# Turning queries, keys, exponentials, gates and outputs on VectorE and the DMA queue instead of TensorE, in a two-layer hybrid decoder

## The chip, the core and the metric

One core of one Trainium2 chip. The metric is the time of one execution on the device, in microseconds. The engines are named as the profile names them: PE (TensorE, matmuls and transposes by matmul), PEld (PE's weight loads), DVE (VectorE), ACT (ScalarE), POOL (GpSimd) and SP (SyncE, which here issues nearly all DMAs, in order, on one queue). Each engine runs its own instructions in one fixed order and waits on semaphores for those of the others.

## The reference

Two decoder layers over 256 positions of width 2048, all in float32. Each layer has a mixer with two kinds of heads that share one input and one output projection, then a SwiGLU feed-forward part (FFN), then a gated embedding per layer (PLE):

```
h = rms_norm(x, pre_mix_gain)
q, k, v, hq, hf, hi, hg = split(h @ w_in)          # 1024, 256, 256, 4 x 1024
attn = rms_norm(window_attention(rope(q), rope(k), v, sinks), attn_gain)
f = lb + (1 - lb) * sigmoid(hf);   k_in = (1 - lb) * sigmoid(-hf)
o = rms_norm(recurrence(silu(hq), k_in, hi, log(f)))  # 8 heads, 128 x 128 states
x += rms_norm(concat(attn, o * silu(hg)) @ w_out, post_mix_gain)
h = rms_norm(x, pre_ffn_gain)
x += rms_norm((silu(h @ w_gate) * (h @ w_up)) @ w_down, post_ffn_gain)
x += (p @ w_ple_proj) * sigmoid(rms_norm(x, ple_gain) @ w_ple_gate)
```

Attention has 16 query heads of 64 on 4 key heads, a window of 128 positions and one sink per head.

## The kernel before

**Strips.** All weights are streamed from DRAM. The unit is a *strip*: 512 columns of a weight matrix for all 256 positions, as two row tiles t = 0, 1 of 128 positions, each with an accumulator in PSUM (`acc0`, `acc1`; four buffers, so two strips). A strip of 2048 inputs comes in 8 chunks of 512 KB: `load_w` (L232) brings a chunk into `wr` (4 buffers), ACT casts it to a high part `wh` (L174), DVE makes the low part `wl` by subtraction (L175; 8 buffers of each, so one strip), and PE does 12 matmuls of 128x512 with it, 6 for each row tile: high times high (L251), low input times high (L252), high input times low (L254). So a strip is 96 matmuls. In the text below, "matmul 480" counts these weight matmuls from the start of a layer; the first layer's mixer has its strips at 0 (keys and values), 96 and 192 (queries q0, q1), then twice f, q_rec, i, g (the recurrence's two groups of heads): 288, 384, 480, 576 and 672, 768, 864, 960; from 1056 come the output projection (`w_out`), FFN and PLE. The second layer begins at 5040.

**What a strip leaves.** When a row tile is complete, `done(t, ps)` reads it from PSUM: for queries DVE multiplies it by sines and cosines (L472) and POOL adds (L479); for f, ACT writes z (L616); for q_rec ACT writes a sigmoid (L635) and DVE the product (L636), both into a `nat` buffer; g likewise (L801 to L804). The `acc` buffer of a strip is written again by the strip two places later, whose first matmul waits for these reads.

**Turning.** The next step mostly needs the data turned (positions along the free axis). Before, PE does that: four transposes by matmul with `ident` into a PSUM bank `ms` (L491 keys, L511 queries, L571 exponentials, L621 z, L644 q_rec, L189 in `split_T` for attention output, recurrence output and new x), and ACT or DVE reads the bank. In the FFN only, `shuffled` (L204) turns the hidden tile by DVE and DMAs: one DVE transpose of 32x32 blocks (L208), one DMA of 256 KB to a DRAM buffer `turn` (L211), and four DMAs of 64 KB that read the blocks back in their places (L214); `split_shuffled` then splits the result into its high and low part.

**What sets the order.** The program is written as strips in a row. `tick()` runs once a chunk; it advances the generators (attention, the recurrence's levels) by one `yield` and runs what `later(n, f)` left for n ticks hence. So the number of `yield`s and the n of `later` set after which chunk a step is issued; the tile framework's scheduler then orders each engine's instructions by priority and by when buffers and inputs come free, and puts the waits in. Engines do not reorder. SP carries the weight loads, and the turns between them.

**Attention** (`attend`, `head_pair`): per half and row tile the rotated queries are turned, scores computed (L535), then per group of four heads copied (L546) and masked (L547), reduced to the maximum (L550, L551), exponentiated by ACT four times (L554) and once for the sink (L558); the exponentials are turned and multiplied with the values (L586), the result scaled (L589).

Of the kernel before, what the change touches and what calls it, by code (L numbers as in the profile page):

```python
# [15 lines left out]
P = 128  # L16
# [30 lines left out]
def decoder(ctx: ExitStack, tc: tile.TileContext, x, p, positions, w_in, attn_sinks,  # L47
# [10 lines left out]
    np_ = ctx.enter_context(tc.tile_pool(name="np", bufs=6))  # L58
# [145 lines left out]
    def shuffled(src):  # L204


        b = nat()
        V.transpose(b.rearrange("p (q k j) -> p k q j", q=4, k=4),  # L208
                    src.rearrange("p (k q j) -> p k q j", k=4, q=4))
        m = dp.tile([4, 32, 4, P], F32, tag="turn", name="turn")  # L210
        nc.sync.dma_start(m.rearrange("a i q f -> (a i) (q f)"), b)  # L211
        d = nat()
        for q in range(4):
            nc.sync.dma_start(d[q * 32:(q + 1) * 32].rearrange("i (a f) -> i a f", a=4),  # L214
                              m[:, :, q].rearrange("a i f -> i a f"))
        return d

    def split_shuffled(d, hl, t):
        cols = slice(t * P, (t + 1) * P)
        split(d.rearrange("p (a k j) -> p k a j", a=4, k=4),  # L220
              *(a[:, :, cols].rearrange("p k (a j) -> p k a j", a=4) for a in hl))
# [223 lines left out]
    for l in range(DEPTH):  # L445
# [35 lines left out]
        def done_kv(t, ps):  # L481
# [6 lines left out]
            def turn():  # L488
                pt = bank((P, 2, P))
                for b in range(2):  # L490
                    T.transpose(pt[:, b], o[:, b * P:(b + 1) * P], ident)  # L491
                S.copy(kT[:, :, t * P:(t + 1) * P], pt)
            later(8 - t, turn)
# [12 lines left out]
        def attend(half, t, o):  # L506
            for _ in range(3):
                yield
            pt = bank((P, 4, P))
            for b in range(4):  # L510
                T.transpose(pt[:, b], o[:, b * P:(b + 1) * P], ident)  # L511
            S.copy(qT[half][:, :, t * P:(t + 1) * P], pt)
            yield
            yield from head_pair(half, t)
            if half == 1:
# [4 lines left out]
                yield  # L520
                for h in range(2):
                    split_T(blocks4(ao[t][:, h]), gain_cols(96, l, 8)[:, 4 * h:4 * h + 4], attn[h], t)

        def head_pair(half, t):
# [13 lines left out]
            for g in range(2):  # L538
# [22 lines left out]
                ex.append(s_)  # L561
# [6 lines left out]
            def turned(g):  # L568
                pt = bank((P, 4, P))
                for j in range(4):  # L570
                    T.transpose(pt[:, j], ex[g][:, j], ident)  # L571
                ec = nat((P, 4, P))
                if t == 0:
                    S.copy(ec, pt)
                    return [(t, ec)]
                ep = nat((P, 4, P))
                V.tensor_tensor(ec, pt, m_low.unsqueeze(1).to_broadcast([P, 4, P]), op=ALU.mult)
                V.tensor_tensor(ep, pt, m_up.unsqueeze(1).to_broadcast([P, 4, P]), op=ALU.mult)
# [23 lines left out]
        class Rec:  # L602
# [11 lines left out]
            def done_f(s, t, ps):  # L614
                z = nat()
                S.activation(z, ps, AF.Copy, scale=rx(t)[:, 0:1])  # L616

                def turn():
                    pt = bank((P, 4, P))
# [11 lines left out]
                later(2, turn)  # L631

            def done_q(s, t, ps):
# [6 lines left out]

                def turn():
                    pt = bank((P, 4, P))
                    for b in range(4):
                        T.transpose(pt[:, b], sg[:, b * P:(b + 1) * P], ident)  # L644
                    raw = s.qd[:, :, t, 0:P]
                    cols = slice(t * P, (t + 1) * P)
                    S.copy(raw, pt)
# [8 lines left out]
                later(3 - t, turn)  # L656
# [142 lines left out]
            def done_g(s, t, ps):  # L799
# [163 lines left out]
```

## Time and profile before

| | |
|---|---|
| median of 3 runs | 2468.09 us (2467.95 to 2470.01) |
| profiled execution | 2468.36 us |
| its span, first to last instruction | 2466.6 us, at a mean granted clock of 0.999 |
| moved by DMA | 472.40 MB, mean 192 GB/s, the queues' share 63.1% |
| weight chunks | 840 (176 for w_in, 64 w_out, 3 x 176 FFN, 64 PLE gate, 8 PLE projection), 3.8 to 4.5 us from issue to landing |
| turns (FFN only) | 40: out 256 KB, 2.7 us to landing; back 4 x 64 KB, 3.3 us |
| PSUM banks | 4 `acc`, 4 `ms` |

How to read the rows quoted below. A row of the timeline has the start and the duration in us, the engine, the line, the operation, output and inputs, the shape, and a count where equal rows were joined; in brackets the idle time before it and what ended it. A row of groups has line, engine, operation, tiles and shapes with a count, then busy us and mean ns of one, then the idle time of the engine just before them and its releaser. Matmuls are pipelined: their durations overlap, so the pace is read from their starts. A row of waits has the engine and line, what it waited for, then us in total, times, and the longest. A row of windows has for each engine the busy time and (instructions), then the granted clock of PE as a share of full speed, the DMA share and GB/s.

### The profile page before, as it was taken

What the parts mean: (1) busy time and instruction counts of PE and PEld (TensorE: products, weight loads), DVE (VectorE), ACT (ScalarE), POOL (GpSimd) and SP (SyncE); (2) the same over time, 40 slices, a digit from 0 to 9 for tenths busy, and PEclk for the clock granted to TensorE, in tenths of its full rate; (3) what the DMA queues carried; (4) which work ended last, traced back from release to release, by engine and by line L of the source; (5) the groups of instructions that cost most, each with busy time, mean ns of one, the idle gap of its engine ahead of it and who ended that gap; (6) DMA issues with size and microseconds to landing.
All of it is one profiled execution on the core that took longest, in us unless ns stands there. A gap on an engine that the chain in (4) does not pass through costs nothing.

```text
span 2466.6 us, 30888 instructions
## 1 busy us (share of the span) xinstructions
PE 2447.2 (99%) x11437; PEld 2023.1 (82%) x11437; DVE 1465.8 (59%) x1941; ACT 1186.8 (48%) x1684; POOL 101.2 (4%) x213
## 2 busy tenths in 40 slices
PE   8999999999999999999999999999999999999999
PEld 6888887888888888887888888878888888888877
DVE  7786756545555555557566867565455555555674
ACT  6655446444434444446556444464444444444463
POOL 3100001000000000001010000010000000000010
PEclk9999999999999999999999999999999999999999
DMA  8445565767667766765564454657677676677753
GB/s 258 141 142 161 153 189 162 233 192 207 215 206 209 213 209 197 225 221 158 185 202 141 139 169 144 200 173 220 189 212 222 197 212 210 209 211 211 222 173 126
DMA packets 263062, 472.40 MB, mean 192 GB/s; under 512 B 17376, under 2 KB 38784, under 8 KB 262912
## 3 DMA queue, kind: packets, MB, share of 16 engines
q1 hardware_dynamic: 262608, 470.36, 63.1%
q8 instruction: 89, 1.46, 0.2%
q14 instruction: 61, 0.50, 0.1%
q10 hardware_dynamic: 240, 0.07, 0.0%
q0 software_dynamic: 64, 0.02, 0.0%
HBM read 457.79 MB, written 12.58 MB: 191 GB/s over the span
## 4 chain that ended last, share of the span: by engine, by line
PE 95%; DMA 2%; DVE 1%; ACT 1%; issue 0%; POOL 0%; SPq 0%; ACTq 0%; DVEq 0%; POOLq 0%
PE acc L251 30%; PE acc L252 30%; PE acc L254 29%; DMA wr<-in_w_in_dram 1%; PE ms L696 1%; PE ms L586 1%; PE ms L189 1%; DVE wl L175 1%; PE ms L535 0%; ACT wh L174 0%; PE ms L733 0%; ACT junk L170 0%; PE ms L761 0%; PE ms L254 0%; PE ms L251 0%
## 5 line engine op out<-in xcount | busy, mean ns | idle before, releaser
L175 DVE TENSOR_TENSOR wl<-wr,wh 128x1024 fp32r<-128x1024 f32 x840 | 1026.8, 1224 | 897.1 <-ACT wh L174 884.1
L174 ACT CAST wh<-wr 128x1024 fp32r<-128x1024 f32 x840 | 883.9, 1054 | 1096.0 <-PE acc L252 1004.8
L251 PE MATMUL acc<-wh,ck 128*128 128x512 f32 x3328 | 1305.9, 393 | 9.2 <-ACT ck L200 5.8
L252 PE MATMUL acc<-wh,ck 128*128 128x512 f32 x3328 | 1299.1, 391 | 1.0 <-DVE ck L201 1.0
L254 PE MATMUL acc<-wl,ck 128*128 128x512 f32 x3328 | 1296.3, 390 | 0.0
L251 PEld LDWEIGHTS acc<-wh,ck 128*128 128x128 f32 x3328 | 625.1, 188 | 143.2 <-ACT ck L200 11.4
L252 PEld LDWEIGHTS acc<-wh,ck 128*128 128x128 f32 x3328 | 625.7, 188 | 133.5 <-DVE ck L201 4.9
L254 PEld LDWEIGHTS acc<-wl,ck 128*128 128x128 f32 x3328 | 624.8, 188 | 129.5
L200 ACT ACTIVATE ck<-ms,gT 128x128 fp32r<-128x128 f32 x248 | 78.9, 368 | 36.3 <-DVE ck L201 28.4
L201 DVE SCALAR_TENSOR_TENSOR ck<-ms,gT,ck 128x128 fp32r<-128x128 f32 x248 | 75.9, 346 | 20.5 <-ACT ck L200 19.9
L160 POOL TENSOR_TENSOR tiny<-ssf 128x1 f32<-128x1 f32 x4 | 2.1, 535 | 1361.2 <-ACT junk L170 1360.9
L887 DVE TENSOR_TENSOR macc<-acc,macc 128x512 f32<-128x512 f32 x48 | 33.0, 687 | 5.1 <-PE acc L254 4.5
L857 ACT ACTIVATE nat<-acc,ry 128x512 f32<-128x512 f32 x44 | 30.2, 686 | 10.7 <-PE acc L254 10.7
L170 ACT ACTIVATE junk<-x 128x512 f32<-128x512 f32 x48 | 30.3, 631 | 6.4 <-DVE x L286 4.1
L863 DVE SCALAR_TENSOR_TENSOR nat<-acc,ry,nat 128x512 f32<-128x512 f32 x44 | 32.4, 748 | 0.1
L189 PE MATMUL ms<-ident,x 128*128 128x128 f32 x192 | 27.8, 280 | 1.7 <-DVE x L920 1.3
L189 PEld LDWEIGHTS ms<-ident,x 128*128 128x128 f32 x192 | 22.6, 143 | 8.1 <-DVE x L920 2.4
L175 DVE TENSOR_TENSOR ck<-nat,ck 128x512 fp32r<-128x512 f32 x42 | 28.8, 686 | 0.0
L208 DVE STREAM_TRANSPOSE nat<-nat 128x512 f32<-128x512 f32 x40 | 28.1, 703 | 0.0
L174 ACT CAST ck<-nat 128x512 fp32r<-128x512 f32 x42 | 26.0, 619 | 4.0 <-DVE nat L181 3.6
L479 POOL TENSOR_TENSOR nat<-nat 128x256 f32<-128x256 f32 (+1 forms) x24 | 22.8, 973 | 106.6 <-DVE nat L472 50.2
L554 ACT ACTIVATE nat<-nat,tiny 128x128 f32<-128x128 f32 x64 | 24.8, 389 | 3.9 <-DVE tiny L551 3.6
(199 smaller groups left out, 871.0 us busy)
## 6 DMA issues: line engine op xcount, KB each, us to landing
wr<-in_w_in_dram SPq DMA_DIRECT2D x176, 512.0 KB, 3.8
wr<-in_w_ffn_gate_dram SPq DMA_DIRECT2D x176, 512.0 KB, 4.4
wr<-in_w_ffn_up_dram SPq DMA_DIRECT2D x176, 512.0 KB, 4.5
wr<-in_w_ffn_down_dram SPq DMA_DIRECT2D x176, 512.0 KB, 4.3
wr<-in_w_out_dram SPq DMA_DIRECT2D x64, 512.0 KB, 3.9
wr<-in_w_ple_gate_dram SPq DMA_DIRECT2D x64, 512.0 KB, 4.3
turn<-nat SPq DMA_DIRECT2D x40, 256.0 KB, 2.7
nat<-turn SPq DMA_DIRECT2D x160, 64.0 KB, 3.3
```

The costliest lines, as they stand in the source:

```text
L170: S.activation(j[:, 0:shape[1]], src, AF.Square, accum_out=acc)
L174: a = S.copy(hi, src)
L175: v = V.tensor_tensor(lo, src, hi.bitcast(F32), op=ALU.subtract)
L189: T.transpose(ps[:, b], blk, ident)
L200: marks["x"] = S.activation(h[:, b], ps[:, b], AF.Copy, scale=g)
L201: V.scalar_tensor_tensor(lo[:, b], ps[:, b], g, h[:, b].bitcast(F32), op0=ALU.mult, op1=ALU.subtract)
L251: T.matmul(ps[t], xh, hi[:, k], start=first, stop=False)
L252: T.matmul(ps[t], xl, hi[:, k], start=False, stop=False)
L254: marks[t, c] = T.matmul(ps[t], xh, lo[:, k], start=False, stop=last)
L857: S.activation(gate[t], ps, AF.Silu, scale=rx2(t)[:, 0:1])
L863: V.scalar_tensor_tensor(gate[t], ps, rx2(t)[:, 0:1], gate[t], op0=ALU.mult, op1=ALU.mult)
L887: V.tensor_tensor(m, ps, m, op=ALU.add)
```

## The change

`shuffled` takes a width of n blocks and returns the turned tile as a view of blocks, and 66 more tiles go through it instead of PE: the keys (4, n = 2), the rotated queries (8), the exponentials (16), z of f (8), the gate and query product of q_rec (8), the attention output (8), the recurrence's output (8), and in the first layer three of the four column blocks of the new x (6). The turns rise from 40 to 106, and 256 PE transposes go (10984 PE matmuls before, 10728 after). The readers of the turned tiles (copies, masks, sigmoids, splits with gain) now read `nat` buffers in SBUF instead of PSUM. Steps are issued some ticks later: queries 5 ticks after the rotation instead of 3, z 4 instead of 2, q_rec 5 - t instead of 3 - t, attention output 5 instead of 1, recurrence output 4 instead of 2, the new x 5 - t instead of 2 - t; in `head_pair` a `yield` moves ahead of the masking. `nat` has 9 buffers instead of 6. The lines of the changed file are 2 to 11 higher than those before in the parts quoted (L251, L252, L254 become L261, L262, L264).

```diff
-    np_ = ctx.enter_context(tc.tile_pool(name="np", bufs=6))
+    np_ = ctx.enter_context(tc.tile_pool(name="np", bufs=9))
...
-    def shuffled(src):
+    def shuffled(src, n=4):
-        b = nat()
-        V.transpose(b.rearrange("p (q k j) -> p k q j", q=4, k=4),
-                    src.rearrange("p (k q j) -> p k q j", k=4, q=4))
-        m = dp.tile([4, 32, 4, P], F32, tag="turn", name="turn")
+        b = nat((P, n * P))
+        V.transpose(b.rearrange("p (q k j) -> p k q j", q=4, k=n),
+                    src.rearrange("p (k q j) -> p k q j", k=n, q=4))
+        m = dp.tile([4, 32, 4, n * 32], F32, tag="turn", name="turn")
         nc.sync.dma_start(m.rearrange("a i q f -> (a i) (q f)"), b)
-        d = nat()
+        d = nat((P, n * P))
         for q in range(4):
             nc.sync.dma_start(d[q * 32:(q + 1) * 32].rearrange("i (a f) -> i a f", a=4),
                               m[:, :, q].rearrange("a i f -> i a f"))
-        return d
+        return d.rearrange("p (a k j) -> p k a j", a=4, k=n)
...
+    def split_shuffled(d, gcols, hl, t):
+        h, lo = (quarters(a[:, :, t * P:(t + 1) * P]) for a in hl)
+        if gcols is None:
+            split(d, h, lo)
+            return
+        for b in range(4):
+            g = gcols[:, b:b + 1]
+            marks["x"] = S.activation(h[:, b], d[:, b], AF.Copy, scale=g)
+            V.scalar_tensor_tensor(lo[:, b], d[:, b], g, h[:, b].bitcast(F32),
+                                   op0=ALU.mult, op1=ALU.subtract)
...
         def attend(half, t, o):
-            for _ in range(3):
+            d = shuffled(o)
+            for _ in range(5):
                 yield
-            pt = bank((P, 4, P))
-            for b in range(4):
-                T.transpose(pt[:, b], o[:, b * P:(b + 1) * P], ident)
-            S.copy(qT[half][:, :, t * P:(t + 1) * P], pt)
+            S.copy(quarters(qT[half][:, :, t * P:(t + 1) * P]), d)
             yield
             yield from head_pair(half, t)
...
-                yield
+                d = [shuffled(ao[t][:, h]) for h in range(2)]
+                for _ in range(5):
+                    yield
                 for h in range(2):
-                    split_T(blocks4(ao[t][:, h]), gain_cols(96, l, 8)[:, 4 * h:4 * h + 4], attn[h], t)
+                    split_shuffled(d[h], gain_cols(96, l, 8)[:, 4 * h:4 * h + 4], attn[h], t)
...
-                ex.append(s_)
+                ex.append(shuffled(s_.rearrange("p j k -> p (j k)")))
...
-            p0 = turned(0)
             yield
+            p0 = masked(0)
             yield
             values(0, p0)
-            p1 = turned(1)
-            yield
+            p1 = masked(1)
             yield
             values(1, p1)
...
                 z = nat()
                 S.activation(z, ps, AF.Copy, scale=rx(t)[:, 0:1])
+                d = shuffled(z)
                 def turn():
-                    pt = bank((P, 4, P))
-                    for b in range(4):
-                        T.transpose(pt[:, b], z[:, b * P:(b + 1) * P], ident)
                     cols = slice(t * P, (t + 1) * P)
-                    S.activation(s.f[:, :, cols], pt, AF.Sigmoid)
-                    S.activation(s.k[:, :, cols], pt, AF.Sigmoid, scale=-1.0)
+                    S.activation(quarters(s.f[:, :, cols]), d, AF.Sigmoid)
+                    S.activation(quarters(s.k[:, :, cols]), d, AF.Sigmoid, scale=-1.0)
...
-                later(2, turn)
+                later(4, turn)
...
-                later(3 - t, turn)
+                later(5 - t, turn)
...
-                later(2, lambda: split_T(blocks4(o), gain_cols(112, l, 8)[:, 4 * s.grp:4 * s.grp + 4],
-                                         mix[c], t))
+                d = shuffled(o)
+                later(4, lambda: split_shuffled(d, gain_cols(112, l, 8)[:, 4 * s.grp:4 * s.grp + 4],
+                                                mix[c], t))
...
+                    d = shuffled(xr[t][s]) if s < 3 else None
                     def turn(xT=nxT, ss=nss, g=gain_cols(0, l + 1, 16)):
-                        next_in(t, s, xT, g)
+                        if s < 3:
+                            split_shuffled(d, g[:, 4 * s:4 * s + 4], xT[s], t)
+                        else:
+                            next_in(t, s, xT, g)
                         square_sum(xr[t][s], ss[t][:, s:s + 1])
-                    later(3 if s == 3 else 2 - t, turn)
+                    later(3 if s == 3 else 5 - t, turn)
```

**Where instructions move, first place.** ACT's order in the first layer around the reading of z (`nat_1344`, `nat_1367` before; `nat_1408`, `nat_1425` in the changed kernel) from the accumulators of the f strip. Before:

```order
L554 ACTIVATE nat_1264,tiny_1270<-nat_1264,tiny_1267 128x128 x4
L558 ACTIVATE tiny_1275<-tiny_1275 128x4
L574 COPY nat_1303<-ms_1298 128x512
L174 CAST wh_1622<-wr_1620 128x1024
L616 ACTIVATE nat_1344<-acc0_1043,rx0_531 128x512
L174 CAST wh_1640<-wr_1638 128x1024
L574 COPY nat_1365<-ms_1360 128x512
L170 ACTIVATE junk_1358,ssa0_152<-ao0_150 128x256
L616 ACTIVATE nat_1367<-acc1_1044,rx1_557 128x512
```

In the changed kernel, where `wh_1961` is the eighth chunk of the i strip (480 to 576):

```order
L174 CAST wh_1961<-wr_1959 128x1024
L552 COPY nat_1328<-ms_1308 128x512
L560 ACTIVATE nat_1328,tiny_1334<-nat_1328,tiny_1331 128x128 x4
L564 ACTIVATE tiny_1339<-tiny_1339 128x4
L552 COPY nat_1371<-ms_1309 128x512
L560 ACTIVATE nat_1371,tiny_1377<-nat_1371,tiny_1374 128x128 x4
L564 ACTIVATE tiny_1382<-tiny_1382 128x4
L619 ACTIVATE nat_1408<-acc0_1086,rx0_531 128x512
L619 ACTIVATE nat_1425<-acc1_1087,rx1_566 128x512
```

Before, the cast next to z (`wh_1622`, the seventh chunk of the strip after f) takes a buffer that the f strip itself frees. Now the exponentials of q1's second row tile and the cast of `wh_1961` come first, and that cast takes the buffer of the eighth chunk of the q_rec strip, last read by matmul 478.

**Second place.** ACT's order around the sigmoid of q_rec (L635 before, L637 now), first layer. Before:

```order
L200 ACTIVATE ck_144<-ms_1576,gT_101 128x128
L200 ACTIVATE ck_146<-ms_1589,gT_101 128x128
L635 ACTIVATE nat_1650<-acc0_1369,rx0_531 128x512
L174 CAST wh_1899<-wr_1897 128x1024
L635 ACTIVATE nat_1660<-acc1_1370,rx1_557 128x512
```

In the changed kernel (`nat_1573`, `nat_1582`, `nat_1640` and `nat_1649` are the four turned tiles of the attention output; `wh_2213` takes the buffer that matmul 574 frees):

```order
L174 CAST wh_2195<-wr_2193 128x1024
L229 ACTIVATE ck_144<-nat_1573,gT_101 128x128 x4
L174 CAST wh_2213<-wr_2211 128x1024
L229 ACTIVATE ck_146<-nat_1582,gT_101 128x128 x4
L229 ACTIVATE ck_144<-nat_1640,gT_101 128x128 x3
L637 ACTIVATE nat_1702<-acc0_1436,rx0_531 128x512
L229 ACTIVATE ck_144<-nat_1640,gT_101 128x128
L229 ACTIVATE ck_146<-nat_1649,gT_101 128x128 x3
L637 ACTIVATE nat_1721<-acc1_1437,rx1_566 128x512
```

L635 stood behind splits that read PSUM banks; L637 stands behind splits that read tiles brought by DMA, and behind a later cast.

**Third place.** SP's order in the changed kernel between z and the attention output (`turn_1412` and `turn_1429` are z's, `turn_1571` and `turn_1580` the attention output's first two); before, this stretch of SP's order holds weight loads (L232) alone:

```order
L211 DMA turn_1389<-nat_1387 128x512
L214 DMA nat_1391<-turn_1389 32x4x128 x4
L211 DMA turn_1412<-nat_1410 128x512
L214 DMA nat_1414<-turn_1412 32x4x128 x4
L211 DMA turn_1429<-nat_1427 128x512
L242 DMA wr_2124<-in_w_in_dram 128x2x512
L214 DMA nat_1431<-turn_1429 32x4x128 x4
L242 DMA wr_2175<-in_w_in_dram 128x2x512
L242 DMA wr_2193<-in_w_in_dram 128x2x512
L211 DMA turn_1571<-nat_1569 128x512
L214 DMA nat_1573<-turn_1571 32x4x128 x4
L211 DMA turn_1580<-nat_1578 128x512
```

A read (L214) waits for its own turn's L211 to land, and all that is behind it in the queue waits with it.

More of the change, by code (lines that the diff above doesn't have):

```diff
@@ L486, in done_kv @@
             S.activation(vv[:, t], ps[:, 256:512], AF.Copy, scale=rx(t)[:, 0:1])
[L488 to L493, printed above, removed]
+            d = shuffled(o[:, 0:256], 2)
+            later(8 - t, lambda: S.copy(quarters(kT[:, :, t * P:(t + 1) * P]), d))
         def done_q(half):
@@ L639, in done_q @@
                     s.qd = sp.tile([P, 4, NT, P + 64], F32, tag="D", name="qd")
+                d = shuffled(sg)
                 def turn():
-                    pt = bank((P, 4, P))
-                    for b in range(4):
-                        T.transpose(pt[:, b], sg[:, b * P:(b + 1) * P], ident)
                     raw = s.qd[:, :, t, 0:P]
                     cols = slice(t * P, (t + 1) * P)
-                    S.copy(raw, pt)
+                    S.copy(quarters(raw), d)
                     def odd(a):
@@ L868, in done_up @@
                     d = shuffled(gate[t])
-                    later(3, lambda: split_shuffled(d, hl, t))
+                    later(3, lambda: split_shuffled(d, None, hl, t))
                 strip(xT, w_ffn_gate[l], col, done_gate, skew=SKEW if ff0 + j == 0 else 0)
```

19 lines of the change are left out of this document (7 added, 12 removed).

## The prediction

> **What bounds the kernel now.** I read the page first: the busy shares, the granted clock and the chain that ended last, then PE's own waits.
>
> ```profile
> PE 2447.2 (99%) x11437; PEld 2023.1 (82%) x11437; DVE 1465.8 (59%) x1941; ACT 1186.8 (48%) x1684; POOL 101.2 (4%) x213
> ...
> PEclk9999999999999999999999999999999999999999
> ...
> PE 95%; DMA 2%; DVE 1%; ACT 1%; issue 0%; POOL 0%; SPq 0%; ACTq 0%; DVEq 0%; POOLq 0%
> ...
> PE acc L251 <- ACT ck L200: 5.8, 9, 1.3
> PE acc L251 <- ACT wh L174: 3.3, 1, 3.3
> ```
>
> The reader is to see that PE hardly ever waits: 2447.2 of 2466.6 us busy, 95% of the chain, and the two largest of its waits are 5.8 and 3.3 us in all. So whatever leaves PE is a gain in full, and whatever makes PE wait is a loss in full; there is no slack on PE that could hide either. DVE (59%) and ACT (48%) have room in sum. What matters is where, in their fixed order, they stand when PE asks for something.
>
> **What leaves PE.** The order of the changed kernel has 256 PE matmuls fewer, all of them transposes: 62 groups of four and 4 groups of two (the keys). Their price is read from the starts of the neighbours.
>
> ```profile
> 84.17 0.39 PE L251 MATMUL acc<-wh,ck 128*128 128x512 f32 x1
> 84.40 0.39 PE L252 MATMUL acc<-wh,ck 128*128 128x512 f32 x1
> 84.63 0.40 PE L254 MATMUL acc<-wl,ck 128*128 128x512 f32 x1
> 84.86 0.60 PE L571 MATMUL ms<-ident,nat 128*128 128x128 f32 x4
> 85.22 0.48 PE L251 MATMUL acc<-wh,ck 128*128 128x512 f32 x1
> 85.54 0.39 PE L252 MATMUL acc<-wh,ck 128*128 128x512 f32 x1
> ...
> 62.49 0.40 PE L251 MATMUL acc<-wh,ck 128*128 128x512 f32 x1
> 62.72 0.41 PE L491 MATMUL ms<-ident,nat 128*128 128x128 f32 x2
> 62.88 0.48 PE L252 MATMUL acc<-wh,ck 128*128 128x512 f32 x1
> 63.20 0.39 PE L254 MATMUL acc<-wl,ck 128*128 128x512 f32 x1
> ```
>
> Weight matmuls follow each other every 0.228 us (84.17, 84.40, 84.63). With four transposes between, the second matmul after them starts at 85.54; without them it would be 84.63 + 2 x 0.228 = 85.09, so a group of four costs 0.45 us. A group of two costs 63.20 - (62.49 + 2 x 0.228) = 0.25 us. Gain: 62 x 0.45 + 4 x 0.25 = **28.9 us**.
>
> [...]
>
> **What is added, and lies beside PE.** 66 turns: each is one DVE transpose, one DMA out and four DMAs back.
>
> ```profile
> L208 DVE STREAM_TRANSPOSE nat<-nat 128x512 f32<-128x512 f32 x40 | 28.1, 703 | 0.0
> 457.99 0.34 SPq L211 DMA_DIRECT2D turn<-nat  x1
> 459.09 0.37 SPq L232 DMA_DIRECT2D wr<-in_w_ffn_up_dram  x1
> 461.17 1.76 SPq L214 DMA_DIRECT2D nat<-turn  x4
> DMA to landing us min/median/max: 1.8/3.3/6.2
> ```
>
> DVE: 62 x 0.703 + 4 x about 0.36 = 45 us, which takes it from 59% to 61%. SP: a turn is issued at 457.99, its last read at 461.17 + 1.76 = 462.9, so a turn holds the queue some 4.9 us (with one weight load in between; I take 4.6 without it), and its data are there about 2 us after that. This lies beside PE wherever nobody asks for it sooner. I cost the keys, both outputs of the recurrence, the new x and the second recurrence group at nothing: the matmuls until their reader hide them (the last turned output, `mix[3]`, is read 1128 + 13 matmuls into a layer, 85 matmuls or 19 us behind its strip, against 17 for reading that strip, two turns in series (9.2), their landing and the splits). Were this cover 5 us short, each layer would lose 5 us more. The weight loads between the turns keep their lead: 20 turns of one attention stage are 92 us of SP, and PE takes 87 us for its 384 matmuls before any stall.
>
> **What PE will wait for.** Each `acc` pair is used again two strips later, so a strip of PE cannot start before ACT or DVE has read the strip two before it. In the orders above these reads have moved behind work that itself waits for PE. The durations:
>
> ```profile
> L175 DVE TENSOR_TENSOR wl<-wr,wh 128x1024 fp32r<-128x1024 f32 x840 | 1026.8, 1224 | 897.1 <-ACT wh L174 884.1
> L174 ACT CAST wh<-wr 128x1024 fp32r<-128x1024 f32 x840 | 883.9, 1054 | 1096.0 <-PE acc L252 1004.8
> ...
> L554 ACT ACTIVATE nat<-nat,tiny 128x128 f32<-128x128 f32 x64 | 24.8, 389 | 3.9 <-DVE tiny L551 3.6
> ...
> L546 ACT COPY nat<-ms 128x512 f32<-128x512 f32 x8 | 4.2, 570 | 0.0
> L547 DVE COPY_PREDICATED nat<-m_prev,ms 128x512 f32<-128x512 int32 x8 | 5.5, 736 | 0.4
> L550 DVE TENSOR_REDUCE tiny<-nat 128x4 f32<-128x512 f32 x16 | 10.8, 677 | 0.0
> L616 ACT ACTIVATE nat<-acc,rx 128x512 f32<-128x512 f32 x8 | 5.5, 684 | 3.1 <-PE acc L254 3.1
> L472 DVE TENSOR_TENSOR nat<-acc,rot 128x512 f32<-128x512 f32 x16 | 10.4, 685 | 2.7 <-POOL nat L479 1.9 <-PE acc L254 0.4 <-issue 0.3
> L635 ACT ACTIVATE nat<-acc,rx 128x512 f32<-128x512 f32 x8 | 5.5, 686 | 1.1 <-PE acc L254 1.1
> L636 DVE SCALAR_TENSOR_TENSOR nat<-acc,rx,nat 128x512 f32<-128x512 f32 x8 | 6.0, 745 | 0.0
> L200 ACT ACTIVATE ck<-ms,gT 128x128 fp32r<-128x128 f32 x248 | 78.9, 368 | 36.3 <-DVE ck L201 28.4
> ```
>
> The L174 row says what ACT is doing: 1004.8 us of its idle time end with a matmul, because a cast needs the buffer of eight chunks earlier, one strip. So ACT is never ahead of PE by more than that, and everything behind a cast in its order waits with it. Positions below count a layer's weight matmuls.
>
> *The i strip (480) waits for z.* In the order, `L619` stands behind the cast of `wh_1961`, whose buffer matmul 478 frees. From there: cast 1.05, then on DVE wl 1.22, predicated copy 0.74, reduction 0.68 and a small minimum 0.16, four exponentials 1.55 (they overlap a little), in sum 5.4; then on DVE their transpose 0.70, two small ones 0.34 and again predicated copy, reduction and minimum, 1.58; then four exponentials 1.55, the small one behind them 0.19 and z itself 0.68: 10.4 us, less the two matmuls that PE still has: **10 us**, in either layer. Before, z was read as soon as it was there:
>
> ```profile
> 123.33 0.69 ACT L616 ACTIVATE nat<-acc,rx 128x512 f32<-128x512 f32 x1 [1.07 <-PE acc L254]
> 156.10 0.68 ACT L635 ACTIVATE nat<-acc,rx 128x512 f32<-128x512 f32 x1
> ```
>
> 33 us before PE came to the i strip (which follows the row at 156.10). That slack is what is gone; no transfer is part of this chain, so no DMA speed can mend it.
>
> *The q_rec strip (384) waits for the rotation of q1.* Its two reads (L472, in the changed file L482) stand in DVE's order behind the wl split that matmul 383 releases. In the second layer that is 1.22 + 2 x 0.685 = **2.6 us**; in the first the predicated copy, reduction, exponentials and transpose stand between as well, + 0.74 + 0.68 + 0.16 + 1.55 + 0.19 + 0.70 + 0.34 = 4.4: **7.0 us**.
>
> *The g strip (576) waits for the gate of q_rec.* `L637` stands in ACT's order behind the splits (L229) of the turned attention output. Floor, if every turn has landed: the cast that matmul 574 releases 1.05, seven splits 2.6, L637 0.69, L638 0.75, less 0.46 = 4.6 us. Other end: when the i strip starts, SP has six turns to do, on the last of which L637 waits, in series 6 x 4.6 = 27.6 us, and by the order there are about 9 us of gaps between them, since the attention output can only be scaled and transposed after the values, the sigmoids of f and k and four wl splits on DVE. With the landing (1.8) and the rest (2.5) that is 41 us after the start of the i strip; PE is there after 96 x 0.228 + four groups of values (3.4) + small waits, 27 to 28 us. So 4.6 to 13 us; I take **12**, near the walk's end, as the gaps are instructions with known durations.
>
> *Smaller ones:* values and scores of q1 wait for the turned q1 and exponentials (427 to 436) 3.5 and 2.0 us, the values at 523 to 532 1 us, the rest to 636 1 us per layer; between nothing and twice that.
>
> Per layer: 7.0 + 3.5 + 10 + 1 + 12 + 1 = 34.5 in the first, 2.6 + 2.0 + 10 + 1 + 12 + 1 = 28.6 in the second, **63.1 us**.
>
> **The clock after a stall.** The start of this trace has one long wait:
>
> ```profile
> 9.35 0.80 PE L251 MATMUL acc<-wh,ck 128*128 128x512 f32 x1 [3.31 <-ACT wh L174]
> 9.94 0.63 PE L252 MATMUL acc<-wh,ck 128*128 128x512 f32 x1
> 10.37 0.63 PE L251 MATMUL acc<-wh,ck 128*128 128x512 f32 x1
> ...
> 9.00:12.00 3.00, 2.65 (x6) 2.16 (x7) 2.45 (x2) 1.97 (x4) 2.03 (x35) 0.52 1.04 382
> 12.00:15.00 3.00, 3.00 (x17) 2.51 (x16) 1.36 (x2) 2.78 (x6) 0.00 (x0) 0.91 1.08 346
> ```
>
> After 3.31 us of idling the granted clock is 0.52 and matmuls start every 0.43 us, until 12.5: about eight of them at 0.2 us extra, 1.6 us. What is lost after the stall at 480 only shortens the one at 576, so I count it once per layer: **3.2 us**. [...]
>
> **Sum.** Against the profiled execution, 2468.36 us (span 2466.6 and 1.8 around it): - 28.9 + 63.1 + 3.2 = + 37.4, so 2505.8; the median of the runs is 0.3 lower: **2505.5 us**.
>
> **Rivals.** *Floor only:* turns land in time, 576 costs 4.6 and the small waits vanish: 7.0 + 2.6 + 20 + 9.2 + 3.2 - 28.9 = + 13, 2481 us. The FFN's 40 turns speak for it, on which no row of PE's waits hangs; the six turns in a row speak against it. *Faster:* the casts do not hold ACT and DVE at 383, 478 and 574, because they have run further ahead of PE than one strip when they come to these places; then only transfers are waited for, 4.6 at 576 and about 5 at 427 to 436 and around per layer: 19 - 28.9 = - 10, 2458 us. It decides at the cast before z: is it done before matmul 478 ends? The 1004.8 us above speak against it. *All of the gain*, no new wait: 2439 us; it needs every read of `acc` to be early, which the order contradicts. *Weights starve:* with 6 us per turn (the longest landing was 6.2) 20 turns are 120 us of SP against the stage's 115 (87 and its stalls), and loads behind them come late by some 10 us a layer: 2525 us. That the change doesn't do what it says: the order has no transposes left at these lines.
>
> **Chances.** Forecast 0.52, floor 0.20, faster 0.12, all of the gain 0.05, starving 0.11. The range leaves out the whole gain and the outer part of the last: 2460 to 2526 us. 0.2% (5 us) is about what measurement can tell from no change here: faster 0.15, same 0.05, slower 0.80.
>
> **What would show it.** PE's waits, now 14 us, list `acc` waiting for L619 (about 20 us in two long waits of 10) and for L638 (two of 9 to 13), and L482 in the first layer near 7; the granted clock dips behind each. PE busy falls by about 29. If L619 is not among the waits, the reading of the order is wrong, and the time is below 2470; if PE waits for wh or wl by tens of microseconds, the weights starve.

## The result, and the profile after

| | before | after |
|---|---|---|
| median, each of 4 runs on one chip | 2468.02 us (2467.07 to 2470.01) | 2520.97 us (2518.12 to 2526.50) |
| ratio after to before | | 1.0216, interval 1.0204 to 1.0228 |
| profiled execution, its span | 2468.36, 2466.6 us | 2519.89, 2518.2 us |
| mean granted clock | 0.999 | 0.987 |

So the change makes the kernel 2.2% slower; the forecast was 2505.5 with slower as the likeliest side. Of the page of the changed kernel, first the busy times, then the granted clock in 40 slices:

```profile
PE 2439.8 (97%) x11181; PEld 2008.5 (80%) x11181; DVE 1507.0 (60%) x2007; ACT 1189.0 (47%) x1684; POOL 95.9 (4%) x213
...
PEclk9998999999999999999999899999999999999999
```

PE has 256 matmuls fewer and yet only 7.4 us less of busy time (2447.2 before). It idles 2518.2 - 2439.8 = 78 us where it idled 19. Two slices, one in each layer's mixer, have a lower clock. Next PE's waits in the changed kernel (what waits, for what; us in total, times, longest):

```profile
PE acc L261 <- DVE nat L638: 23.3, 2, 11.7
PE acc L261 <- ACT nat L619: 20.6, 2, 10.3
PE acc L261 <- DVE nat L482: 11.2, 2, 7.7
PE acc L261 <- ACT ck L200: 6.1, 9, 1.3
PE acc L261 <- ACT wh L174: 3.1, 1, 3.1
PE ms L541 <- ACT qT L516: 2.2, 2, 1.8
PE acc L261 <- ACT ck L229: 2.2, 2, 1.9
```

The first three rows are new, each with one wait in each layer: 55.1 us together. All waits of this view add up to 73 us, against 14 before: + 59. With PE's - 7.4 that is the whole difference of the spans, + 51.6. No row speaks of late weights (`wh` stands there with its one wait at the start, 3.1 us), so the queue's extra turns did not starve the stream. On the timeline of the changed kernel the waits stand at the first matmuls of the strips at 384, 480 and 576, in the first layer and in the second:

```profile
120.69 0.77 PE L261 MATMUL acc<-wh,ck 128*128 128x512 f32 x1 [7.71 <-DVE nat L482]
...
125.65 0.39 PE L261 MATMUL acc<-wh,ck 128*128 128x512 f32 x1
...
165.25 0.80 PE L261 MATMUL acc<-wh,ck 128*128 128x512 f32 x1 [10.28 <-ACT nat L619]
...
206.53 0.80 PE L261 MATMUL acc<-wh,ck 128*128 128x512 f32 x1 [11.59 <-DVE nat L638]
...
1364.69 0.76 PE L261 MATMUL acc<-wh,ck 128*128 128x512 f32 x1 [3.50 <-DVE nat L482]
...
1409.06 0.79 PE L261 MATMUL acc<-wh,ck 128*128 128x512 f32 x1 [10.28 <-ACT nat L619]
...
1449.84 0.79 PE L261 MATMUL acc<-wh,ck 128*128 128x512 f32 x1 [11.73 <-DVE nat L638]
```

Behind the first of them PE needs 125.65 - 120.69 = 4.96 us for 12 matmuls that take 12 x 0.228 = 2.74 at full pace: 2.2 us more are lost after the wait has ended. Why z (L619) is late can be read from ACT's own timeline, ahead of the wait that ends at 165.25:

```profile
154.78 1.04 ACT L174 CAST wh<-wr 128x1024 fp32r<-128x1024 f32 x1 [1.67 <-PE acc L262]
155.73 0.58 ACT L552 COPY nat<-ms 128x512 f32<-128x512 f32 x1
158.67 0.40 ACT L560 ACTIVATE nat<-nat,tiny 128x128 f32<-128x128 f32 x1 [2.36 <-DVE tiny L557]
...
160.32 0.56 ACT L552 COPY nat<-ms 128x512 f32<-128x512 f32 x1
162.88 0.40 ACT L560 ACTIVATE nat<-nat,tiny 128x128 f32<-128x128 f32 x1 [2.00 <-DVE tiny L557]
...
164.53 1.47 ACT L619 ACTIVATE nat<-acc,rx 128x512 f32<-128x512 f32 x2
```

This is the chain of the prediction: a cast that waited for PE's own matmul, then two head groups' maxima and exponentials, each of which waits for DVE, and only then the two reads of z, for which PE stands still. The strip whose sums they are had ended at about 113, where PE's wait of 7.71 us begins, 51.5 us earlier; before the change the strip ended at 124.6 and ACT read its first tile at 123.3, as soon as that was complete.

In the FFN, which has the same 40 turns in both kernels, nothing is gained or lost: matmul 1440 of the program starts 28.9 us later than before, and so does matmul 4320. Behind the first layer's PLE, where the new x is turned, it is 26.0 (matmul 5040); the second layer's mixer adds the rest (51.5 at 6240, 51.6 at the last).

### The profile page after: what moved, and what is told of

It is laid out like the page before. It is cut to its first block, busy times and chain, and to the rows that moved or that the text cites. A ratio compares the mean times of both kernels' runs of the same rounds, so it can differ in the third digit from the quotient of the medians.

```text
span 2518.2 us, 30982 instructions
## 1 busy us (share of the span) xinstructions
PE 2439.8 (97%) x11181; PEld 2008.5 (80%) x11181; DVE 1507.0 (60%) x2007; ACT 1189.0 (47%) x1684; POOL 95.9 (4%) x213
## 4 chain that ended last, share of the span: by engine, by line
PE 91%; DMA 3%; ACT 2%; DVE 2%; issue 1%; SPq 0%; POOL 0%; ACTq 0%; DVEq 0%; POOLq 0%
PE acc L261 29%; PE acc L262 29%; PE acc L264 28%; DMA wr<-in_w_in_dram 1%; DMA turn<-nat 1%; PE ms L697 1%; PE ms L590 1%; DMA nat<-turn 1%; DVE wl L175 1%; ACT wh L174 1%; PE ms L541 1%; ACT nat L560 0%; PE ms L734 0%; PE ms L189 0%; ACT junk L170 0%
## 5 line engine op out<-in xcount | busy, mean ns | idle before, releaser
L175 DVE TENSOR_TENSOR wl<-wr,wh 128x1024 fp32r<-128x1024 f32 x840 | 1025.1, 1224 | 853.5 <-ACT wh L174 850.4
L261 PE MATMUL acc<-wh,ck 128*128 128x512 f32 x3328 | 1307.6, 394 | 67.0 <-DVE nat L638 23.3
L262 PE MATMUL acc<-wh,ck 128*128 128x512 f32 x3328 | 1304.6, 392 | 0.9 <-DVE ck L201 0.8
L264 PE MATMUL acc<-wl,ck 128*128 128x512 f32 x3328 | 1299.7, 391 | 0.0
L261 PEld LDWEIGHTS acc<-wh,ck 128*128 128x128 f32 x3328 | 628.1, 189 | 209.1 <-DVE nat L638 24.2
L262 PEld LDWEIGHTS acc<-wh,ck 128*128 128x128 f32 x3328 | 628.7, 189 | 135.8 <-DVE ck L201 5.0
L264 PEld LDWEIGHTS acc<-wl,ck 128*128 128x128 f32 x3328 | 627.4, 189 | 129.5
L208 DVE STREAM_TRANSPOSE nat<-nat 128x512 f32<-128x512 f32 (+1 forms) x84 | 58.2, 693 | 38.3 <-ACT nat L560 22.6
L200 ACT ACTIVATE ck<-ms,gT 128x128 fp32r<-128x128 f32 x160 | 50.2, 370 | 14.8 <-DVE ck L201 7.0
L201 DVE SCALAR_TENSOR_TENSOR ck<-ms,gT,ck 128x128 fp32r<-128x128 f32 x160 | 48.4, 346 | 14.0 <-ACT ck L200 13.6
L229 ACT ACTIVATE ck<-nat,gT 128x128 fp32r<-128x128 f32 x88 | 28.5, 390 | 32.3 <-DMA nat<-turn 32.3
L230 DVE SCALAR_TENSOR_TENSOR ck<-nat,gT,ck 128x128 fp32r<-128x128 f32 x88 | 26.3, 349 | 20.3 <-ACT ck L229 20.3
L859 ACT ACTIVATE nat<-acc,ry 128x512 f32<-128x512 f32 x44 | 30.2, 687 | 10.7 <-PE acc L264 10.7
L175 DVE TENSOR_TENSOR ck<-nat,ck 128x512 fp32r<-128x512 f32 x42 | 28.9, 687 | 0.1
```

Of the source, the lines that this page charges most:

```text
L175: v = V.tensor_tensor(lo, src, hi.bitcast(F32), op=ALU.subtract)
L200: marks["x"] = S.activation(h[:, b], ps[:, b], AF.Copy, scale=g)
L201: V.scalar_tensor_tensor(lo[:, b], ps[:, b], g, h[:, b].bitcast(F32), op0=ALU.mult, op1=ALU.subtract)
L208: V.transpose(b.rearrange("p (q k j) -> p k q j", q=4, k=n), src.rearrange("p (k q j) -> p k q j", k=n, q=4))
L261: T.matmul(ps[t], xh, hi[:, k], start=first, stop=False)
L262: T.matmul(ps[t], xl, hi[:, k], start=False, stop=False)
```

## The experiments

In these kernels a string chooses which of the added turns are made: K keys, Q queries, E exponentials, Z z, S gate and query product, A attention output, H recurrence output, X new x. A tile whose letter is missing is turned by PE, with the ticks of the kernel before; with no string shown, all are turned. All compute the whole reference. Intervals are of the ratio to the kernel before, whose median was 2468.6 us on each of the three chips used.

**The exponentials back on PE.** If the length of the chain ahead of z is the cause, taking the turn (and its two buffers) out of that chain must bring z forward.

```diff
+TURN = "KQZSAHX"
...
-                ex.append(shuffled(s_.rearrange("p j k -> p (j k)")))
+                ex.append(shuffled(s_.rearrange("p j k -> p (j k)")) if "E" in TURN else s_)
```

> Exponentials back on PE (16 turns fewer), all else as changed. By its order z now stands behind the cast that matmul 394 releases, no longer 478. Theory (PE waits at strip starts for reads that stand late in ACT's and DVE's order, and each wait costs a clock restart): the two waits of 10.3 us for z go, the rotation's 7.7 goes to about nothing, the two for q_rec's gate of 11.7 fall to 2 to 5, six clock restarts of 1.5 to 2.2 mostly go, 16 groups of 0.45 come back: about 2465 us (2458 to 2476). Rival 1 (the turns in series on SP's queue are the cause): z's chain has no transfer, so its 20.6 stay: about 2495. Rival 2 (more DVE work and DMA traffic slow everything, in proportion to the turns): 16 of 66 turns of the 82 us that the gain of 29 hides, less the gain given back: about 2508.

Measured 2464.85 us (2461.84 to 2467.51), 0.9984 [0.9974, 0.9993]: 56 us less than the changed kernel, with 16 of the 66 turns gone. Of its waits of PE:

```profile
PE acc L262 <- DVE nat L862: 4.1, 2, 2.5
...
PE acc L262 <- DVE nat L691: 1.2, 1, 1.2
```

The waits for z (now L665) and for the rotation are gone, the one for the gate (L691) is 1.2 us, and the longest new one is 2.5 us, for the recurrence's output gate (L862). So without the exponentials' turns there is no loss; the other 50 turns keep 3.8 us of the 21.7 that 46 groups of four and 4 of two are worth at the predicted prices.

**Is it the turn, or its buffers?** A turn takes two `nat` buffers beside its source: `b`, which DVE writes and the DMA reads, and `d`, into which the data come back. They can be one, since the DMAs back wait for the DMA out in any case:

```diff
-        d = nat((P, n * P))
+        d = b
```

The second kernel has this too, and splits the nine buffers: seven `nat`, and two of a tag of their own for the reads of `acc` (z, and the gate's product of q_rec).

```diff
-    np_ = ctx.enter_context(tc.tile_pool(name="np", bufs=9))
+    np_ = ctx.enter_context(tc.tile_pool(name="np", bufs=7))
...
-                z = nat()
+                z = np_.tile([P, W], F32, tag="zq", name="zq", bufs=2)
...
-                sg = nat()
+                sg = np_.tile([P, W], F32, tag="zq", name="zq", bufs=2)
```

> All turns as changed, but the data read back land in the buffer that was written out (d is b), so a turn holds one nat buffer less; still nine shared ones. By its order z stands behind the cast that matmul 442 releases. Theory: z's wait falls from 10.3 to 0 to 4, the gate's to about 6, some new waits for values: about 2488 us (2478 to 2500). Rivals 1 and 2: the same turns on the same queue, same work and traffic: 2520 us, as the changed kernel.

> As the one before (d is b), with the same nine buffers split: seven shared, two for z and q_rec's product alone. By its order z stands behind the cast that matmul 346 releases. Theory: no wait for z and none for the gate over 2 us; values and the g strip's end wait 3 to 4: about 2480 us (2470 to 2488), some 8 us under the shared nine. Rivals 1 and 2: 2520 us, no difference to the shared nine.

Measured 2489.48 us, 1.0081 [1.0066, 1.0096], with nine shared buffers, and 2458.87 us, 0.996 [0.9946, 0.9974], with seven and two: the second expectation missed, by 11 us below its lower end. Both have all 66 turns, on the same queue, and the same memory.

The first one met its time, but only in part as expected. z is waited for once (2.9), and the gate not at all, where about 6 were expected. In place of that PE waits for values (L613) and, longest, for casts of weights:

```profile
PE acc L262 <- ACT wh L175: 15.3, 3, 6.8
PE ms L626 <- ACT nat L613: 7.4, 3, 3.2
```

One of those three is the wait at the start; the others are 6.8 and 5.6 us, one in each layer. PE, ACT and the SP queue at the first of them:

```profile
186.97 0.79 PE L262 MATMUL acc<-wh,ck 128*128 128x512 f32 x1 [6.80 <-ACT wh L175]
...
185.88 1.04 ACT L175 CAST wh<-wr 128x1024 fp32r<-128x1024 f32 x1 [2.99 <-DMA wr<-in_w_in_dram]
...
172.10 7.73 SPq L215 DMA_DIRECT2D nat<-turn  x16
```

The cast waits for its weights. SP issued no weight load from 156.7 to 180.8, while six turns stood in its order, the sixteen reads of four of them in a row (in the second layer none from 1387.3 to 1409.5). That is the "weights starve" of the prediction: absent from the changed kernel, present in this one.

The split kernel's first read of z, on ACT's timeline:

```profile
108.46 0.68 ACT L665 ACTIVATE zq<-acc,rx 128x512 f32<-128x512 f32 x1
```

And of its waits of PE:

```profile
PE acc L265 <- DVE wl L176: 4.7, 2, 2.4
PE acc L262 <- DVE nat L862: 3.7, 2, 1.9
```

z is read at 108.46 where the changed kernel read it at 164.53, and neither z nor the gate of q_rec is waited for; no wait but the one at the start is above 2.5 us. The 62 us between the split and the changed kernel (31.5 for one buffer less in each turn, 30.6 for the split) are therefore not the price of transposing on DVE, nor of 66 turns on the queue as such: the buffers decide where the reads of `acc` stand, and when the turns come. The queue is not free even so. ACT's casts wait for chunks of `w_in` 7.4 us in the kernel before, 28.0 in the changed one, 61.6 with one buffer a turn and 83.3 in the split kernel, where no wait of PE for `wh` is left but the one at the start. What the orders and the profiles of six kernels say together, for the first layer (the row of the exponentials alone is an experiment further down):

| kernel | `nat` buffers, new ones per turn | turns added | z stands in ACT's order behind the cast released by matmul | f's strip ends at, us | first z read at, us | longest wait for z, us |
|---|---|---|---|---|---|---|
| before | 6, none in the mixer | 0 | 370 | 124.6 | 123.3 | none |
| changed | 9, two | 66 | 478 | 113.0 | 164.5 | 10.28 |
| exponentials on PE | 9, two | 50 | 394 | 116.2 | 132.4 | none |
| exponentials alone | 9, two | 16 | 478 | 114.5 | 152.9 | none |
| one buffer a turn | 9, one | 66 | 442 | 120.9 | 150.3 | 2.9 |
| one a turn, z apart | 7 and 2, one | 66 | 346 | 109.5 | 108.5 | none |

(A first tile is complete a little before its strip ends.) With shared buffers, z stands the later in the order, the more buffers the exponentials' turns ahead of it take: behind 478 with two each, behind 442 with one, behind 394 with none, read 51.5, 29.4 and 16.2 us after its strip's end. The number of turns does not decide: 16 turns of exponentials alone put z as far back as all 66 do. Where z has buffers of its own it is read at once. More `nat` buffers than nine were not tried.

**Only z, the recurrence's output and new x turned** (22 turns, none of them in the attention):

```diff
+TURN = "ZHX"
```

> Only z, the recurrence's output and the new x are turned on DVE and DMA (22 turns), all else on PE as before. By its order z stands behind the cast that matmul 370 releases, as before. Theory: no new wait, 22 groups of 0.45 us: 9.9 us under the kernel before, 2458 us (2455 to 2462). Rival 2 (cost in proportion to the turns, 82 us for 66): 27 us of cost less 9.9: about 2485 us. Rival 1: turns here are seldom in series: 2458 to 2465.

Measured 2457.57 us, 0.9955 [0.994, 0.997]. Its span is 2455.9, 10.7 us under that of before, where 22 groups of four at the predicted 0.45 give 9.9. PE's waits are 12.6 us in all, against 14. So the price of a group of transposes on PE, which the changed kernel's busy time hides, was right.

**Only the exponentials turned** (16 turns, nine buffers):

```diff
+TURN = "E"
```

> Exponentials alone are turned on DVE and DMA (16 turns, nine shared buffers), all else on PE. By its order z stands behind the cast that matmul 478 releases, as in the changed kernel. Theory: 16 groups of 0.45 come off (7.2 us), but PE waits at the end of the q_rec strip and the start of the i strip for values and z, 6 to 10 us a layer, with a clock restart of 1.5 to 2.2 each: 2478 us (2470 to 2486), slower than the kernel before. If the exponentials' turns need the other parts to do harm (longer series of turns), it is faster: 2462 us.

Missed: 2491.64 us, 1.0094 [1.0079, 1.0109], 5.6 us above the upper end. PE's longest wait is for the turned exponentials (L613):

```profile
PE ms L626 <- ACT nat L613: 12.2, 2, 6.1
```

On PE's timeline it ends at 153.06, and the `values` matmuls (L626) that follow are these; below them is ACT's first read of z:

```profile
153.06 1.97 PE L626 MATMUL ms<-vv,nat 128*128 128x64 f32 x8 [6.11 <-ACT nat L613]
154.79 0.77 PE L262 MATMUL acc<-wh,ck 128*128 128x512 f32 x1
155.36 5.29 PE L626 MATMUL ms<-vv,nat 128*128 128x64 f32 x24
...
152.91 0.68 ACT L665 ACTIVATE nat<-acc,rx 128x512 f32<-128x512 f32 x1
```

z is read 38.4 us after its strip's end, as late as its place in the order says, and still no wait of PE is for it: PE stands at the values first, and when these have come and been used, z's first tile has been read as well.

Windows of 3 us, with the granted clock as the third number from the end:

```profile
154.00:157.00 3.00, 3.00 (x15) 2.90 (x14) 1.37 (x3) 0.68 (x2) 0.00 (x0) 0.50 0.40 135
...
160.00:163.00 3.00, 3.00 (x12) 2.62 (x12) 2.31 (x5) 1.46 (x5) 0.19 (x1) 0.50 0.01 2
...
166.00:169.00 3.00, 3.00 (x24) 2.83 (x24) 1.57 (x6) 1.77 (x6) 0.15 (x1) 1.00 0.00 0
```

The wait is 6.1 us, at the lower end of what was expected; what was not expected is that the clock then stays at 0.50 until about 165, through nearly 7 us of busy PE on 32 small matmuls. An estimate from these windows: from 154 to 163 half of 9 us is lost, some 4.5 us, and 1 more to 166, in each layer. The account of the span (+ 24.4): 16 groups less - 7.2, waits 25.8 - 14 = + 11.8, and PE's busy time 19.4 above what that leaves, of which these stretches are 11. The other 8 are not accounted for.

**The reads of each turn on another queue.** The prediction explained the wait at 576 by six turns in series on SP. Here the four DMAs back go to POOL's queue:

```diff
-            nc.sync.dma_start(d[q * 32:(q + 1) * 32].rearrange("i (a f) -> i a f", a=4),
+            nc.gpsimd.dma_start(d[q * 32:(q + 1) * 32].rearrange("i (a f) -> i a f", a=4),
```

> The changed kernel with the four reads of each turn issued by GpSimd's queue, so that writes and weight loads no longer stand behind reads on SP. By its order z stands behind the cast that matmul 478 releases, as in the changed kernel. Theory: the two waits of 10.3 for z stay, as their chain holds no transfer; the gate's 11.7 falls only by what the series of turns on SP was worth: 5 to 12 us; 2505 to 2530 us with what GpSimd's own work loses. Rival 1 (SP's queue is the cause): z's and the gate's waits both fall to under 4: about 2480 us.

Measured 2564.48 us, 1.0389 [1.0368, 1.041] (two runs). The waits for z stay, 10.27 in the first layer, and the one for the gate falls from 11.59 to 7.05, as expected; the total is 34 us above the range. PE's timeline:

```profile
169.82 0.79 PE L262 MATMUL acc<-wh,ck 128*128 128x512 f32 x1 [10.27 <-ACT nat L665]
...
207.06 0.79 PE L262 MATMUL acc<-wh,ck 128*128 128x512 f32 x1 [7.05 <-DVE nat L691]
```

Of PE's waits:

```profile
PE acc L262 <- ACT ck L175: 14.7, 9, 3.0
PE acc L262 <- DVE nat L691: 14.3, 3, 7.1
```

And of the groups of instructions, POOL's DMA issues:

```profile
L215 POOL DMA_DIRECT2D nat<-turn x424 | 231.1, 552 | 1558.0 <-DMA turn<-nat 736.5 <-DVE wl L176 568.4 <-DVE nat L209 205.5
```

An issue holds POOL for 552 ns, 231 us in all, and all 106 turns pay it, the FFN's 40 included: there stand the 14.7 us of waits for L175. So it is no cheaper way, and what turns in series are worth it shows only roughly: the gate's wait fell by 4.5 of 11.6 us, but in this kernel ACT reads the gate's first tile (204.59) behind two turned tiles of the attention output, in the changed kernel behind most of a third one as well. PE's busy time is 17.8 us above the changed kernel's; about half of that is slow clock (105 weight matmuls at the half pace, 60 in the changed kernel), the rest was not taken apart.

**What remains to be had.** The split buffers, with the turns that are asked for soonest left on PE: the exponentials, the exponentials and queries, or keys as well.

```diff
+TURN = "KQZSAHX"
...
+TURN = "KZSAHX"
...
+TURN = "ZSAHX"
```

> The split buffers of the run before last but one (d is b, seven shared, two for z and q_rec's product), exponentials back on PE, 50 turns. By its order z stands behind the cast that matmul 370 releases, the gate's read behind 466. Theory: against the 2458.9 of all 66 turns with these buffers, 16 groups come back (7.2 us), the waits for wl (4.7) and for the g strip's read (3.7) shrink: 2457 us (2450 to 2463). Rival 2 (cost in proportion to turns): it has been refuted by the runs so far unless this comes out below 2445.

> Split buffers (seven shared, two for z and q_rec's product; d is b); queries and exponentials on PE, the 42 other turns on DVE and DMA. By its order z stands behind the cast that matmul 370 releases. Theory: 38 groups of four and 4 of two, 18.1 us, less 1 to 4 of small waits: 2452 us (2449 to 2457), level with the version that turns the queries too.

> Split buffers; keys, queries and exponentials on PE, the 38 other turns (z, gate and query product, attention output, recurrence output, new x) on DVE and DMA. By its order z stands behind the cast that matmul 370 releases, the gate's read behind 454. Theory: no wait over 2 us, so 38 groups of 0.45 us come off: 17 us, less up to 4 of small waits: 2454 us (2450 to 2459). Rival (queue): the attention output's four turns in series still delay something by 5 or more a layer: 2462 us.

Measured, in this order: 2451.05 us (2450.70 to 2452.03), 0.993 [0.9915, 0.9945]; 2452.49 (2448.41 to 2453.33), 0.9931 [0.9914, 0.9947]; 2453.29 (2451.09 to 2455.18), 0.9935 [0.9919, 0.9952]. All three beat both kernels; they can't be told apart from each other. The first one's busy times on the page:

```profile
PE 2427.5 (99%) x11245; PEld 2004.9 (82%) x11245; DVE 1488.9 (61%) x1991; ACT 1187.2 (48%) x1684; POOL 102.5 (4%) x213
```

And its two largest waits of PE:

```profile
PE acc L262 <- ACT wh L175: 5.1, 3, 2.9
PE acc L262 <- ACT ck L201: 4.7, 7, 1.1
```

PE waits 15.8 us in all, nearly as before (14), and its busy time is 19.7 us lower, where 46 groups of four and 4 of two at the predicted prices give 21.7. The 16 turns of the exponentials, on top, would be worth 7.2 us on PE; in the split kernel they cost 7.8 net (2458.87 against 2451.05).

## Why the prediction was right, point by point

| step of the prediction | predicted, us (1st, 2nd layer) | measured, us |
|---|---|---|
| strip 384 waits for the rotation (L482) | 7.0, 2.6 | 7.71, 3.50 |
| strip 480 waits for z (L619) | 10, 10 | 10.28, 10.28 |
| strip 576 waits for the gate (L638) | 12, 12 | 11.59, 11.73 |
| smaller waits, both layers | 9.5 | 3.1 (L541 1.75 and 0.48, L590 0.48, two of 0.2) |
| end of the output projection, L229, second layer | covered | 1.91 |
| clock after waits | 3.2 | 12.6 |
| transposes off PE | - 28.9 | - 28.9 at the price that the run with 22 turns bears out, and + 8.9 in PE's busy time elsewhere |

*The waits* were read rightly, in place and in size: the reads of `acc` stand in a fixed order behind casts that wait for PE, and the walk from the cast gave 10 us against 10.28. The floor rival fell (576 took 11.6, not 4.6), and so did "faster" and "all of the gain": the cast ahead of z did wait for PE, as the ACT timeline shows. Starving did not come in this kernel either.

*Why z stands there* the prediction did not ask. It took the order as given; the orders above show that it moves with the buffers, and that the same 66 turns with z apart are 0.4% faster than before. The mechanism "the reads of `acc` are late in the order" is shown, and so is that a change of buffers alone moves them. That the scheduler puts them there because a `nat` buffer is not free fits all six kernels of the table, but is not shown directly: no run tells which buffer z took.

*The wait at 576* was right in size and in its chain. The prediction had the gate's read behind turned tiles of the attention output, the last of six turns in series on SP, and let it end 41 us after the start of the i strip; it ended after 206.53 - 165.25 = 41.3 (40.8 in the second layer), of which in the first PE took 29.7 where 27 to 28 were predicted. ACT's timeline of the changed kernel says what the gate's read stood behind; below it is that of the split kernel, which has the same turns on SP and no such wait:

```profile
204.12 1.00 ACT L229 ACTIVATE ck<-nat,gT 128x128 fp32r<-128x128 f32 x3 [4.25 <-DMA nat<-turn]
205.03 0.67 ACT L637 ACTIVATE nat<-acc,rx 128x512 f32<-128x512 f32 x1
```

```profile
152.28 0.69 ACT L690 ACTIVATE zq<-acc,rx 128x512 f32<-128x512 f32 x1
...
184.14 1.28 ACT L230 ACTIVATE ck<-nat,gT 128x128 fp32r<-128x128 f32 x4 [0.75 <-DMA nat<-turn]
```

In the changed kernel the last link is a turn, as predicted (4.25 us for `nat<-turn`). In the split kernel the turned tiles of the attention output come later still against the strips: the last of them is split at 184.14, after the g strip has begun at 168.68. PE does not wait, because the gate's reads have buffers of their own and stand ahead of these splits, at 152.28 and 153.90. So turns in series make the wait only where a read of `acc` stands behind them; as for z, it is the place in the order that decides.

*The clock* is the term that was mis-sized: 3.2 us, once per layer, against 12.6. The prediction held that what is lost after the stall at 480 only shortens the next one. So it counted one stretch a layer where there are three. The one behind 384 can't shorten the wait at 480, since that wait's chain begins with a cast that PE's own matmul 478 releases. Whether the one behind 480 shortened the wait at 576 these runs do not settle; in the chain there some casts wait for PE and other links for turns. All six long waits and the one of 1.91 us were followed by a slow stretch: 2.2, 2.1, 2.0, 1.5, 1.5, 1.6 and 1.7 us above the pace of 0.228 a matmul. The windows around the wait at 165.25 (the granted clock is the third number from the end):

```profile
165.00:167.50 2.50, 2.25 (x5) 1.84 (x6) 1.16 (x5) 0.88 (x2) 0.00 (x0) 0.50 0.47 159
167.50:170.00 2.50, 2.50 (x8) 1.94 (x7) 0.64 (x1) 0.00 (x0) 0.00 (x0) 0.57 0.30 87
170.00:172.50 2.50, 2.50 (x13) 2.02 (x12) 0.00 (x0) 0.00 (x0) 0.00 (x0) 1.00 0.36 131
```

The clock is back at about 169.7, after some 4 us of PE work at 0.50.

*The gain* on PE was right by the run with 22 turns (10.7 us of span for 9.9). In the changed kernel PE's busy time fell by 7.4, not by 28.9: 12.6 is the clock, and 4.3 stand in the scores: the 192 matmuls of L535 keep PE busy for 12.9 us before, the same of L541 for 17.2 after, at 280 and 281 ns of one. Why they cost more there, and where the last 4.6 us stand, was not settled.

*The sum.* 2505.8 was predicted for the profiled execution, 2519.9 came: waits 4.2 less than predicted (58.9 for 63.1), the clock 9.4 more, the rest of PE 8.9 more; together + 14.1.

## What to carry to other kernels

A step moved from the bounding engine to idle ones costs what it holds, not only what it runs: here each turn held two buffers of a pool into which the accumulators were also read, and these reads slid behind work that waited for the bounding engine itself. Let a step hold as few buffers as it can (31.5 us here), give a read that frees an accumulator buffers of its own (30.6 us more, with no instruction less), and look in each engine's order for what such a read now stands behind. Move off first what is asked for late, and leave on the bounding engine what is asked for at once.

## What the runs showed of the hardware that was not expected

- The clock fell after shorter waits than the 3.31 us of the kernel before, and length alone does not decide it. In the traces of the kernel before and of the changed one the granted clock is 1.00 or 0.50 and, within a trace, changes only at times that lie a whole number of 3.413 us apart (in the changed kernel it is 0.50 from 1613.50 to 1616.91, one such stretch, and from 196.97 to 210.62, four). What went with a fall is how much PE did between two such times. The wait of 1.91 us that ends at 1612.25 in the changed kernel lies inside one stretch; the wait of 1.86 us that ends at 1420.91 in the split kernel lies across a border (in the rows PE's busy time stands behind the stretch's length, the clock third from the end):

```profile
1610.09:1613.50 3.41, 1.50 (x7) 1.05 (x6) 2.40 (x6) 1.71 (x6) 0.00 (x0) 1.00 0.92 320
1613.50:1616.91 3.41, 3.41 (x9) 2.65 (x8) 0.80 (x1) 1.19 (x3) 0.00 (x0) 0.50 0.13 45
```

```profile
1416.75:1420.16 3.41, 2.30 (x12) 1.69 (x10) 3.41 (x14) 2.74 (x3) 0.00 (x0) 1.00 0.22 83
1420.16:1423.57 3.41, 2.66 (x12) 2.19 (x13) 3.41 (x6) 0.00 (x0) 0.00 (x0) 1.00 0.00 0
1423.57:1426.98 3.41, 3.41 (x19) 2.99 (x18) 3.37 (x7) 0.54 (x1) 0.00 (x0) 1.00 0.81 216
```

From 20 us on, each of the 7 full-clock stretches of the changed kernel in which PE was busy for 44% or less was followed by half clock; of its 705 others, busy for 49% or more, none was, nor was any of the 714 of the kernel before, busy for 62% or more.

- The clock did not come back under `values` matmuls of 128x64: 0.50 for 14 us (151 to 165) in the run with only exponentials, PE busy in the last 12 of them, and the same in its second layer (0.50 at 1387, at full clock again at about 1400.6); with one buffer a turn it stayed at 0.50 for 10 us from 110.4 in the first layer, PE busy throughout. In all three places it came back at the end of the first 3.41 us that weight matmuls of 128x512 filled, but for 0.3 us at most. What it was in the small matmuls (their size, or gaps too short for the trace) was not tried.
